# A two-layer decoder trunk: the comparison before a seldom-needed second path becomes a jump, and four engines get a branch hint

## The chip, the cores and the metric

The kernel runs on one core of one Trainium2 chip. The metric is the device time of one execution in microseconds (us). A core has five engines, each with an instruction stream of its own: TensorE (PE in the profile, with its weight loads as PEld), VectorE (DVE), ScalarE (ACT), GpSimd (POOL) and SyncE (SP). Names with a q at the end (SPq, DVEq, PEldq) are the engines' sequencers, which issue DMAs, wait on semaphores, load registers and branch.

## The reference, cut to what matters

`reference()` runs two pre-norm residual layers over 1024 tokens of width 1024, each followed by a SwiGLU feed-forward block, and a final RMSNorm. Layer 0 mixes tokens by a Conformer convolution and an mLSTM; layer 1 by gated linear attention:

```python
for l in range(DEPTH):                      # DEPTH = 2
    h = rmsnorm(x, mix_norm_g[l])
    if l % 2 == 0:
        x = x + conv_mlstm_mixer(h, ...)
    else:
        x = x + gla_mixer(h, ...)           # S_t = diag(alpha_t) S_{t-1} + k_t^T v_t, o_t = q_t S_t
    h = rmsnorm(x, ffn_norm_g[l])
    x = x + swiglu(h, ffn_w1[l], ffn_w3[l], ffn_w2[l])
return rmsnorm(x, final_norm_g)
```

The decays alpha_t of layer 1 come from the data. Their running sums of logarithms decide which of two ways of computing layer 1 can be used.

## The kernel before, in words

Everything is float32, carried by pairs of a rounded value and its remainder, so that each product is three matmuls (`mm3`, L174 to L176). The sequence is cut in two halves of 512 tokens; activations lie as 8 tiles of 128 features by 512 tokens. The feed-forward blocks use a seven-product scheme for 2x2 blocks. The order of the work within an engine comes from the Tile scheduler, steered by priorities and by the lists `ORDER0`, `ORDER1`, `FIRST` and `REST`.

The program is one long straight piece, with a branch near its end:

- `layer(0, mixer0, ...)` (L1844) computes layer 0, and its `done` writes the layer's result to `x1` in DRAM.
- `layer(1, ... mixer1_at_once ...)` (L1845) computes layer 1 under the assumption that the decays of a chunk of 128 tokens stay above a bound. `compare()` (L1058 to L1066) tests that and leaves 1 or 0 in the one-element tile `fits`. The final norm is done by `finish` (L1764) for the first 768 tokens and by `last_tokens` (L1774) for the last 256, whose output is stored at L1834 and L1837 by DMAs on SP's and ACT's queues.
- `nc.values_load(fits, ...)` (L1846) loads `fits` into a register on all five engines (TENSOR_LOAD in the profile).
- `with tc.If(ok < 1, preferred_fallthrough_block=False)` (L1847): if the assumption fails, layer 1 is computed again from `x1` by the slower `mixer1`, and the output is overwritten. This is the long arm. With the given inputs `fits` is 1, and the long arm doesn't run.

An `If` has two arms. The short arm, which the code doesn't write, holds what keeps the semaphores' counts alike on both ways: on PE, DVE, ACT and POOL one semaphore instruction each, on SP eight, one for each of the eight DMA semaphores that this program uses in turn. Each waits until that semaphore has the count of all work issued so far, and then adds what the long arm would have added. On SP these eight thus wait until the last output DMAs have landed. All of them carry L1847 in the profile.

Behind both arms comes the end of the program, under L1971 (the line that closes the `TileContext`): on SP eight waits and a drain, then a barrier of all five engines led by POOL, which clears the semaphores, and a second barrier.

Before the change the streams lie in memory as: straight piece, short arm, long arm, end. An engine for which `fits` is 1 does not jump at the comparison, runs the short arm, and jumps from there over the long arm to the end. Both the comparison and that jump appear as COMPARE_BRANCH under L1847.

Of the kernel before, what the change touches and what calls it, by code (L numbers as in the profile page):

```python
# [79 lines left out]
def trunk_kernel(ctx, tc, xT, cols, gate_b0, ev_vo0, ev_u, ev_cw, ev_out, od_v0, od_u, od_out, gate_w2, fin_row,  # L80
# [57 lines left out]
    def xy(i, half):  # L138
        return hp.tile([P, HALF], F32, tag=f"xy{i}_{half}", name=nm(f"xy{i}"))
# [86 lines left out]
    def norm_half(xs, gc, half):  # L226
        r = rstd_half(xs)
        hs, work = [], []
        for k in range(KT):
            f = tmp()  # L230
            a = DVE.scalar_tensor_tensor(out=f, in0=xs[k], scalar=c1(gc + k), in1=r, op0=ALU.mult, op1=ALU.mult)
            d = hl(k, half)
            work += [[a], [split(d, f, DVE)]]
            hs.append(d)
        return hs, work
# [18 lines left out]
    def out_proj(wd, x_src):  # L254

        ys = [[None] * KT, [None] * KT]
        second = []

        def cut(y, half, ks=range(KT)):
            for k in ks:  # L260
                if ys[half][k] is None:
                    ys[half][k] = hl(k, half)
                    y(k, half, ys[half][k], second if half and k >= 2 else None)

        def run(y, half, done, mp=None):
            if half == 0:
                cut(y, 0)
            x = []
            for i in range(KT):
                w = spare(wd[i], mp) if mp and i in XW else weights(wd[i], 1024, DVE, off=OOFF)  # L270
                if half == 0 and i == 1:
                    second[:] = made
                t = xy(i, half)
                SP.dma_start(t, x_src[i, half])
                x.append(t)
                b = proj(w, ys, half)
                DVE.tensor_tensor(out=t, in0=t, in1=b, op=ALU.add)
            if half == 0:
                cut(y, 1)
            with tc.high_priority(offset=NOFF):  # L280
                done(x, half)
        return run, cut
# [1444 lines left out]
    def layer(l, mixer, w_out, x_src, g, done):  # L1727
        hv, d = ffn_in(g)
        run, cut = out_proj(w_out, x_src)
        ys = []  # L1730

        def then(y, mp):
            ys.append(y)
            run(y, 0, d, mp if l == 0 else None)

        mixer(cut, then)
        with tc.tile_pool(name=f"u{l}", bufs=1, reuse_waits="tile") as fp:
            pools.append(fp)
            run(ys[0], 1, d)
            ffn_up(l, hv, fp)  # L1740
            ffn_down(l, fp, done)
# [101 lines left out]
    h1, b1, done = before(C_MIX + 8)  # L1843
    layer(0, mixer0, ev_out, xT, C_FFN, done)  # L1844
    layer(1, lambda cut, then: mixer1_at_once(h1, b1, cut, then), od_out, x1, C_FFN + 8, finish)  # L1845
    ok = nc.values_load(fits, min_val=0, max_val=1, skip_runtime_bounds_check_because="a comparison gives 0 or 1")  # L1846
    with tc.If(ok < 1, preferred_fallthrough_block=False):  # L1847
        h = []
        for half in range(2):
            xs = [xy(k, half) for k in range(KT)]  # L1850
            for k in range(KT):
                SP.dma_start(xs[k], x1[k, half])
            h.append(norm_half(xs, C_MIX + 8, half)[0])
        layer(1, lambda cut, then: mixer1(h, cut, then), od_out, x1, C_FFN + 8, finish)
# [96 lines left out]
def _build(a):  # L1951
    import concourse.bacc as bacc

    nc = bacc.Bacc("TRN2", target_bir_lowering=False, num_devices=1, dynamic_dma_scratch_size=2048)
    args = [nc.dram_tensor(f"in_{k}", v.shape, mybir.dt.from_np(v.dtype), kind="ExternalInput").ap() for k, v in a.items()]
    args.append(nc.dram_tensor("out_0", (KT, 2, P, HALF), F32, kind="ExternalOutput").ap())
    args.append(nc.dram_tensor("xsp", (KT, 2, P, HALF), F32, kind="Internal").ap())
    md = {n: [nc.dram_tensor(f"md{n}_{k}", (P, HALF), F32, kind="Internal").ap() for k in range(11)]
          for n in ("B11", "B21", "B22", "T1", "T2", "T3", "T4")}
    args.append(nc.dram_tensor("rowd", (2, HEADS, T), F32, kind="Internal").ap())  # L1960
    args.append([nc.dram_tensor(f"ud_{k}", (P, PH, NT), F32, kind="Internal").ap() for k in range(4)])
    args.append(nc.dram_tensor("zd", (32, CG, PH, NT), F32, kind="Internal").ap())
    args.append(nc.dram_tensor("ad", (LEAD, 2, P, HALF), F32, kind="Internal").ap())
    args.append(nc.dram_tensor("x1", (KT, 2, P, HALF), F32, kind="Internal").ap())
    args.append(nc.dram_tensor("cd", (8, 2, P, HALF), F32, kind="Internal").ap())
    args.append(nc.dram_tensor("cv", (2, P, HALF), F32, kind="Internal").ap())
    args.append(nc.dram_tensor("td", (3, 4, P, HALF), F32, kind="Internal").ap())
    args.append(nc.dram_tensor("vd", (2, 2, P, 1024), F32, kind="Internal").ap())
    args.append(nc.dram_tensor("yd", (4, 2, P, HALF), F32, kind="Internal").ap())
    args.append(nc.dram_tensor("bd", (HEADS, 2, P, HALF), F32, kind="Internal").ap())  # L1970
    with tile.TileContext(nc, schedule_with_timeline_sim=True) as tc:  # L1971
        trunk_kernel(tc, *args, md)
    return nc
# [14 lines left out]
```

## Time and profile before

| what | us |
|---|---|
| median of 3 runs | 2112.68 |
| lowest and highest | 2112.63, 2113.97 |
| the profiled execution's own time | 2114.76 |
| its span, first to last instruction of the program | 2113.0 |

| engine | busy us | share of the span | instructions |
|---|---|---|---|
| PE | 2094.4 | 99% | 10367 |
| DVE | 1508.1 | 71% | 2296 |
| ACT | 866.7 | 41% | 1411 |
| POOL | 2.9 | 0% | 15 |

Busy time counts compute instructions alone: semaphore waits, register loads, branches and DMA issues are not in it. A row of a line's view gives engine, operation and count, the shortest, median and longest duration in ns, and where the first and the last of them start, in us from the start of the span. A row of the DMA view gives a queue, its kind, packets, MB and the share of 16 DMA engines' time; the queues of the kind "instruction" bring in the engines' own code.

### The profile page before, as it was taken

The page shows a single profiled execution, that of the slowest core. Times are in us where ns is not written, and L with a number is a line of the kernel's source. Part 1 is how long each engine was busy: PE and PEld are TensorE (multiplying, and loading weights), DVE is VectorE, ACT ScalarE, POOL GpSimd, SP SyncE. Part 2 cuts the span into 40 slices and gives each one's busy share as a digit, 9 for nine tenths or more (in the row PEclk, how much of TensorE's full clock was granted, in tenths as well). Part 3 has the DMA queues.
Part 4 walks back from the last instruction along what each step waited for, and adds up shares of the span by engine and source line. Part 5 has one row for each costly group of instructions (what it writes and reads, how often), then busy time and mean ns, then how long its engine had stood idle before and what let it go on. Part 6 is the DMA issues. An engine that isn't in the chain of part 4 may idle for free.

```text
span 2113.0 us, 27851 instructions
## 1 busy us (share of the span) xinstructions
PE 2094.4 (99%) x10367; PEld 1773.1 (84%) x10367; DVE 1508.1 (71%) x2296; ACT 866.7 (41%) x1411; POOL 2.9 (0%) x15
## 2 busy tenths in 40 slices
PE   9999999999999999999999999999999999999998
PEld 8889989888888888888889978888888888888887
DVE  7555788677776666867876577667877666677696
ACT  6302327443222222444546546744522222235553
POOL 0000000000000000000000000000000000000000
PEclk9999999999999999999999999999999999999999
DMA  4233453555443233834436643554544333374334
GB/s 162 91 107 126 148 131 119 204 170 180 163 157 105 90 113 134 287 97 138 161 127 229 200 141 115 175 184 140 195 155 164 113 116 103 103 285 129 98 122 146
DMA packets 154640, 312.61 MB, mean 148 GB/s; under 512 B 24128, under 2 KB 37312, under 8 KB 154496
## 3 DMA queue, kind: packets, MB, share of 16 engines
q1 hardware_dynamic: 154224, 310.48, 43.9%
q8 instruction: 84, 1.38, 0.3%
q14 instruction: 60, 0.49, 0.1%
q10 hardware_dynamic: 272, 0.26, 0.0%
HBM read 229.91 MB, written 80.77 MB: 147 GB/s over the span
## 4 chain that ended last, share of the span: by engine, by line
PE 94%; DVE 2%; ACT 2%; DMA 1%; issue 0%; SPq 0%; DVEq 0%; ACTq 0%
PE mm L174 20%; PE mm L175 20%; PE mm L176 20%; PE sm L175 10%; PE sm L176 10%; PE sm L174 10%; PE sm L411 2%; PE sm L1266 1%; PE sm L1268 1%; PE sm L1265 1%; DVE bs L1053 0%; DVE hL L147 0%; DVE wL L168 0%; PE sm L1254 0%; PE sm L1293 0%
## 5 line engine op out<-in xcount | busy, mean ns | idle before, releaser
L175 PE MATMUL mm<-hL,wH 128*128 128x512 f32 x1356 | 531.2, 392 | 0.2 <-DVE hL L339 0.2
L176 PE MATMUL mm<-hH,wH 128*128 128x512 f32 x1356 | 529.1, 391 | 0.0
L174 PE MATMUL mm<-hH,wL 128*128 128x512 f32 x1356 | 492.5, 392 | 2.4 <-DVE wL L168 1.4
L174 PEld LDWEIGHTS mm<-hH,wL 128*128 128x128 f32 x1356 | 254.3, 188 | 57.6 <-ACT hH L338 1.3
L175 PEld LDWEIGHTS mm<-hL,wH 128*128 128x128 f32 x1356 | 254.7, 188 | 53.3 <-DVE hL L339 1.0
L176 PEld LDWEIGHTS mm<-hH,wH 128*128 128x128 f32 x1356 | 254.7, 188 | 53.1 <-issue 0.2
L175 PE MATMUL sm<-hL,wH 128*128 128x512 f32 x616 | 240.1, 390 | 0.0
L176 PE MATMUL sm<-hH,wH 128*128 128x512 f32 x616 | 239.7, 389 | 0.0
L174 PE MATMUL sm<-hH,wL 128*128 128x512 f32 x616 | 209.0, 390 | 0.0
L147 ACT ACTIVATE wH<-S 128x1024 fp32r<-128x1024 f32 x97 | 102.8, 1060 | 233.8 <-PE sm L176 214.5
L147 ACT ACTIVATE wH<-q 128x512 fp32r<-128x512 f32 x143 | 90.3, 632 | 178.8 <-PE mm L176 101.3
L147 DVE TENSOR_TENSOR wL<-q,wH 128x512 fp32r<-128x512 f32 x143 | 98.5, 689 | 71.5 <-ACT wH L147 71.0
L147 ACT ACTIVATE wH<-raw 128x1024 fp32r<-128x1024 f32 (+1 forms) x90 | 90.0, 1001 | 118.7 <-PE sm L176 67.3
L147 DVE TENSOR_TENSOR wL<-S,wH 128x1024 fp32r<-128x1024 f32 x97 | 118.4, 1221 | 26.3 <-ACT wH L147 26.3
L175 PEld LDWEIGHTS sm<-hL,wH 128*128 128x128 f32 x616 | 115.6, 188 | 24.7 <-issue 0.7
L174 PEld LDWEIGHTS sm<-hH,wL 128*128 128x128 f32 x616 | 115.6, 188 | 24.5 <-PE mm L176 0.5
L175 PE MATMUL mm<-wL,hH 128*128 128x256 f32 (+2 forms) x480 | 136.0, 284 | 0.0
L176 PEld LDWEIGHTS sm<-hH,wH 128*128 128x128 f32 x616 | 115.6, 188 | 24.2 <-issue 0.2
L176 PE MATMUL mm<-wH,hH 128*128 128x256 f32 (+2 forms) x480 | 135.9, 285 | 0.0
L174 PE MATMUL mm<-wH,hL 128*128 128x256 f32 (+2 forms) x480 | 135.8, 286 | 0.1
L1493 DVE TENSOR_TENSOR c<-sm,c 128x512 f32<-128x512 f32 x110 | 75.6, 687 | 72.5 <-PE sm L176 72.5
L147 DVE TENSOR_TENSOR wL<-raw,wH 128x1024 fp32r<-128x1024 f32 (+1 forms) x90 | 103.3, 1149 | 13.9 <-ACT wH L147 13.8
(355 smaller groups left out, 3579.2 us busy)
## 6 DMA issues: line engine op xcount, KB each, us to landing
raw<-in_w SPq DMA_DIRECT2D x108, 512.0 KB
mdT<-c SPq DMA_DIRECT2D x88, 256.0 KB
m<-mdT SPq DMA_DIRECT2D x88, 256.0 KB
mdB<-c SPq DMA_DIRECT2D x66, 256.0 KB
raw<-in_od_u SPq DMA_DIRECT2D x32, 512.0 KB
q<-in_w SPq DMA_DIRECT2D x60, 256.0 KB
m<-mdB SPq DMA_DIRECT2D x55, 256.0 KB
raw<-in_ev_u SPq DMA_DIRECT2D x20, 512.0 KB
```

What stands on the lines that cost most here:

```text
L147: ins = ACT.activation(dst[0], src, AF.Copy), lo.tensor_tensor(out=dst[1], in0=src, in1=dst[0], op=ALU.subtract)
L174: return (PE.matmul(o, lt[1], rt[0], start=start and not on, stop=False, skip_group_check=on), PE.matmul(o, lt[0], rt[1], start=False, sto ...
L175: PE.matmul(o, lt[0], rt[1], start=False, stop=False, skip_group_check=on),
L176: PE.matmul(o, lt[0], rt[0], start=False, stop=stop, skip_group_check=on))
L411: PE.matmul(o, w[:, m * P:(m + 1) * P], raw[:, e, m:m + NT], start=m == 0, stop=m == SH)
L1265: PE.matmul(db[:, cc, :], kw[:, cs], v[:, c, :], start=True, stop=True)
L1266: PE.matmul(ob[:, cc, :], A[:, cs], v[:, c, :], start=True, stop=st is None)
L1268: PE.matmul(ob[:, cc, :], q[:, cs], st, start=False, stop=True)
L1493: DVE.tensor_tensor(out=out, in0=a, in1=b, op=ALU.add)
```

## The change

```diff
     layer(0, mixer0, ev_out, xT, C_FFN, done)
     layer(1, lambda cut, then: mixer1_at_once(h1, b1, cut, then), od_out, x1, C_FFN + 8, finish)
+    tc.mark_branch_hint_location("redo", hint="LikelyTaken", engines=[mybir.EngineType.SP, mybir.EngineType.Activation, mybir.EngineType.DVE, mybir.EngineType.PE])
     ok = nc.values_load(fits, min_val=0, max_val=1, skip_runtime_bounds_check_because="a comparison gives 0 or 1")
-    with tc.If(ok < 1, preferred_fallthrough_block=False):
+    with tc.If(ok < 1, preferred_fallthrough_block=True, label="redo"):
         h = []
```

The streams now lie as: straight piece, long arm, short arm, end. The comparison is turned round: an engine for which `fits` is 1 jumps over the long arm to the short arm, and the end follows the short arm directly. On SP, ACT, DVE and PE a BRANCH_PREFETCH_HINT instruction names the comparison's branch and says that it is likely taken. POOL gets none. From here on a line of the changed kernel has a number one higher than before, from L1846 on.

This is the part of SP's stream around the comparison before: the last three output DMAs (L1837, L1834), the load of `fits`, the comparison, the short arm's jump, and the first loads of the long arm. Semaphore instructions are not shown.

```order
L1837 DMA out<-xy_3395_17971 128x2x256
L1834 DMA out<-xy_3397_17977 128x256 x2
L1846 TENSOR_LOAD fits
L1847 COMPARE_AND_BRANCH
L1847 UNCONDITIONAL_BRANCH
L164 DMA raw_18388<-in_od_u 128x1024
L164 DMA raw_18394<-in_od_v 128x1088
```

And this is the same place of SP's stream in the changed kernel.

```order
L1837 DMA out<-xy_3395_17971 128x2x256
L1834 DMA out<-xy_3397_17977 128x256 x2
L1847 TENSOR_LOAD fits
L1848 COMPARE_AND_BRANCH
L164 DMA raw_18392<-in_od_u 128x1024
L164 DMA raw_18398<-in_od_v 128x1088
```

The long arm's first load now follows the comparison. The short arm and its jump have moved behind the long arm, at whose end two jumps now stand in a row where one stood: the long arm's, over the short arm, and the short arm's, whose target is what follows it.

The hint was written ahead of the load of `fits`, but carries no dependency that would hold it there. This piece of the difference is the head of SP's stream.

```order
-L1971 UNCONDITIONAL_BRANCH
+L1972 UNCONDITIONAL_BRANCH
+L1972 BRANCH_PREFETCH_HINT
 L114 DMA col<-in_cols 128x136
 L319 DMA raw_119<-in_ev_u 128x512
```

The hint stands at the very top, ahead of the first DMA, and likewise ahead of the first instruction of PE, DVE and ACT. Between it and the comparison lies the whole straight piece: some 1800 instructions on SP, 3000 on DVE, 2000 on ACT and 10,200 on PE, each engine's in the order of before.

## The prediction

> **What bounds the kernel now.** I read the page first, then the stage table of the last 33 us, then the two lines of the branch and of the program's end on SP, and the DMA view over the stretch between them. The kernel as a whole is bound by TensorE:
>
> ```profile
> PE 2094.4 (99%) x10367; PEld 1773.1 (84%) x10367; DVE 1508.1 (71%) x2296; ACT 866.7 (41%) x1411; POOL 2.9 (0%) x15
> ```
>
> The change touches none of that work. It touches what comes after it, and the stage table shows how long that is:
>
> ```profile
> 2080.00:2102.90 22.90, 22.87 (x131) 19.80 (x129) 13.18 (x34) 7.26 (x15) 0.00 (x0) 1.00 0.30 97
> 2102.90:2105.30 2.40, 0.00 (x0) 0.00 (x0) 1.41 (x5) 1.70 (x4) 0.00 (x0) 1.00 0.58 193
> 2105.30:2113.00 7.70, 0.00 (x0) 0.00 (x0) 0.00 (x0) 0.00 (x0) 0.00 (x0) 0.58 0.24 77
> ```
>
> The columns after the stretch and its length are the busy us of PE, PEld, DVE, ACT and POOL. TensorE is done at 2102.9 and the last DVE result at 2105.3; then no engine computes for 7.7 us. SP runs through this stretch like this: it loads `fits`, compares, passes five semaphore waits at once, three more after a hold, jumps, and later reaches the end.
>
> ```profile
> L1846 SPq TENSOR_LOAD <-fits x1: 798/798/798, 2105.8 to 2105.8; - x1
> L1847 SPq COMPARE_BRANCH  x1: 49/49/49, 2106.7 to 2106.7; - x1
> L1847 SPq EVENT_SEMAPHORE  x5: 17/17/17, 2106.8 to 2107.1; - x5
> L1847 SPq EVENT_SEMAPHORE  x3: 17/17/17, 2108.6 to 2108.8; - x3
> L1847 SPq COMPARE_BRANCH  x1: 43/43/43, 2108.9 to 2108.9; - x1
> L1971 SPq EVENT_SEMAPHORE  x10: 17/28/28, 2111.6 to 2112.9; - x10
> L1971 SPq DRAIN  x3: 7/7/13, 2112.2 to 2112.5; - x3
> ```
>
> Two pieces of waiting stand out. Between 2107.1 and 2108.6 SP waits for the last output DMAs to land, 1.5 us. Between the jump at 2108.9 (43 ns long) and the first instruction of the end at 2111.6 lie 2.7 us in which SP has nothing to wait for but its own code. The DMA view over 2108.85 to 2111.7 shows that in this time the chip moved instructions and nothing else:
>
> ```profile
> DMA packets 3, 0.02 MB, mean 9 GB/s; under 512 B 0, under 2 KB 0, under 8 KB 0
> q14 instruction: 3, 0.02, 2.7%
> ```
>
> So the jump's 2.7 us are a fetch of code from where the jump goes. The other engines pay the same price at their jumps, earlier:
>
> ```profile
> L1847 PEldq COMPARE_BRANCH  x2: 95/1914/3732, 2099.5 to 2103.1; - x2
> L1847 DVEq COMPARE_BRANCH  x2: 51/53/55, 2105.0 to 2105.4; - x2
> L1847 ACTq COMPARE_BRANCH  x2: 38/43/48, 2106.3 to 2106.4; - x2
> L1971 PEldq DRAIN  x2: 8/40/73, 2106.9 to 2112.6; - x2
> L1971 DVEq DRAIN  x2: 10/25/40, 2109.0 to 2112.5; - x2
> L1971 ACTq DRAIN  x2: 8/44/81, 2109.3 to 2112.5; - x2
> ```
>
> The DMA view over 2103 to 2106.9 shows the code that PE waited for, by another queue:
>
> ```profile
> q8 instruction: 1, 0.02, 1.5%
> ```
>
> PE's jump at 2103.1 is itself 3732 ns long; DVE goes from its jump at 2105.4 to its first drain at 2109.0 (3.5 us after the jump's 51 ns), ACT from 2106.4 to 2109.3 (2.8). All three stand at the final barrier by 2109.3. SP comes there at 2112.2. Its chain, landing wait, jump, fetch, eight waits, barrier, sets the end of the program.
>
> **The change part by part.** The sum is made against the profiled execution (2114.76 us, span 2113.0), which lies 2.08 us above the median of 2112.68; the difference it gives is then taken from the median. About 0.2% (4.2 us) is what a measurement of this kernel can tell from no change.
>
> *The short arm's jump goes away.* Its target now follows it. That a jump to the next instruction costs nothing is borne out by the one at the head of the program: the order has an UNCONDITIONAL_BRANCH under L1971 on SP, while the trace's only rows of L1971 on SP are the semaphore and drain rows above. In SP's chain the eighth wait starts at 2108.8, and the first wait of the end would then follow at the pace of the waits, (2107.1 - 2106.8) / 4 = 0.075 us, at about 2108.9 instead of 2111.6. That is 2.7 us off the path that sets the end, if the arm and the end come in with one fetch.
>
> *The comparison becomes a jump, which needs that fetch.* SP compares at 2106.7. If the hint does what it says, the code is there when SP jumps. The trace has no jump whose target is there already; the nearest rows are a comparison that falls through (49 ns) from below and SP's 2.7 us, or PE's 3.7, from above. I take the low end for the hinted case, since a fetch ahead of time has all of the kernel to hide in. What covers a slower jump is the landing wait: up to 1.5 us on SP cost nothing, because the DMAs land at 2108.6 whenever SP begins to wait. So the low end, and anything up to 1.5 us, has price zero. Without the cover it would count in full.
>
> *What is late next.* With SP's fetch gone, SP stands at the barrier about 0.6 us after 2108.9 (from 2111.6 to 2112.2 above), at 2109.5. With hints the other three are there by about 2106.6 (ACT, which compares at 2106.3). Without hints DVE would fetch from 2105.1 to 2108.6 and ACT from 2106.3 to 2109.1, still ahead of 2109.5. PE compares at 2099.5, while its queue still holds matmuls until 2102.9, and a 3.7 us fetch there ends at 2103.2. POOL has no hint, but has long passed its comparison:
>
> ```profile
> L1847 POOLq COMPARE_BRANCH  x2: 38/42/45, 1324.1 to 1324.3; - x2
> ```
>
> The landing wait is the new bound of the tail, and it is not touched.
>
> *The hints.* One more instruction at the top of four streams, ahead of SP's first DMA, on which the first real matmul depends by way of the loads. The trace has no such instruction. Its bounds are SP's cheapest row (a drain, 7 ns) and its dearest register instruction (the 798 ns load of `fits`); I take 0.05 us, the size of the branch records (43 and 49 ns), which it is nearest to. A cost below nothing is excluded: the first DMA can only move later.
>
> [...]
>
> *The sum.* Minus 2.7, plus 0, plus 0.05: minus 2.65 us. The span would be 2110.35, the profiled execution 2112.1, and the median 2112.68 - 2.65 = 2110.0.
>
> **The rivals.**
>
> *The hint does nothing, the fetch only moves.* Placed some 1800 instructions ahead of SP's comparison, the hint may be forgotten by then. SP then stalls at 2106.7 + 0.05 for 2.7 us, until 2109.45. By then all DMAs have landed, so the eight waits pass at 0.075 us each, 0.6 us in all, and the end begins at 2110.05 instead of 2111.6: 1.55 us gained, 1.5 after the hint's own 0.05, since the fetch now runs beside the landing wait instead of behind it. Time 2111.2. With PE's 3.7 us as the stall the end begins at 2111.05, the gain is 0.5 and the time 2112.2. For it speaks the distance; against it, that the hint names its branch. Chance 0.25. [...]
>
> *No gain at all.* The arm and the end could come in with two fetches instead of one. Then SP stalls again behind the arm, as it does now: with a working hint the time stays at 2112.68 + 0.05 = 2112.7, and without one it is about 2.7 above the previous rival, 2113.9. Against it stand the page's counts of such packets:
>
> ```profile
> q8 instruction: 84, 1.38, 0.3%
> q14 instruction: 60, 0.49, 0.1%
> ```
>
> PE's 84 packets make 1.38 MB for twice 10367 instructions, some 67 bytes each; a q14 packet of 0.49 MB / 60, or 8 KB, then holds about 120 instructions, and the arm and the end on SP are nine and thirteen by the rows above. But a piece can lie across an edge. Chance 0.08. [...]
>
> *Slower: the armed hint takes room from the ordinary fetches.* If the hint makes each sequencer bring in the target at the top and hold it for the whole kernel, less room is left for the code that comes next, and each step to the next piece of code can stall. The 60 packets of q14 belong to SP, DVE and ACT (POOL with its 15 instructions hardly counts), some 20 each. At 2.7 us a stall, 20 stalls cost such an engine 54 us; with DVE idle for 29% of the span most of this would be absorbed, and if a third showed, the time would be 2112.7 + 18 - 2.7 = 2128. It decides from the point where more than 4.2 + 2.7 = 6.9 us show: two of PE's fetches at 3.7 us, or three of DVE's on PE's path. A single mistaken fetch at the top, 2.7 to 3.7 us, would only cancel the gain. Against it: PE's sequencer runs ahead of its engine (it compared 3.4 us before the last matmul ended), which hides most of one stall; and a hint that names one far branch has no reason to act on others. Chance 0.04.
>
> **How the numbers follow.** Forecast with a working hint 0.60; the moved fetch 0.25; no gain 0.08; slower 0.04; the remaining 0.03 for a gain above 4.2 us, for which I know of no mechanism: the whole stretch behind the landing wait is 2113.0 - 2108.6 = 4.4 us, and the waits and barriers stay. The predicted time is that of the likeliest case, 2110.0. The range goes up to 2112.2, the slow bound of the moved fetch, and down to 2109.0, less than the 1.34 us by which the three runs of before lie apart. It leaves out the no-gain, slow and very fast cases, 0.15. All cases but the last two lie within 0.2% of the time before: same 0.93, faster 0.03, slower 0.04.
>
> **What would show it.** In the profile of the changed kernel SP's comparison (now L1848) should be followed within 0.3 us by the first of eight waits; the last wait of the arm and the first of the end (L1972) should lie 0.1 us apart, with no second COMPARE_BRANCH on SP. The landing wait should still end near 2108.6, and the span near 2110.4. If the hint does nothing, the gap of 2.7 us stands right behind the comparison, and the eight waits follow at 0.075 us. If code comes in by two fetches, a gap over 1 us stands between the arm and the end. The slow rival would show in the q8 and q14 counts (well above 84 and 60) and in waits early in the kernel. A tail that begins later than 2105.3, or a gain above 4.2 us, would say that I have the mechanism wrong.

## The result, and the profile after

| | median us | lowest, highest | runs |
|---|---|---|---|
| before | 2114.98 | 2112.63, 2116.32 | 22 |
| changed | 2111.49 | 2109.53, 2114.05 | 22 |

The ratio is 0.9986, with a 95% interval of 0.9980 to 0.9992: between 1.7 and 4.2 us faster, 3.0 us in the middle (the two medians alone lie 3.5 us apart). That is within the 0.2% of the forecast, and clear of zero. The forecast of 2110.0 stood on three runs of before with a median of 2112.68; in the longer comparison before lies 2.3 us higher, so the change is the better measure: -2.65 us forecast, -3.0 measured. The times alone hardly part the forecast from the rival in which the fetch only moves: 2111.49 lies nearer to that rival's 2111.2, and the 1.5 us that it would gain lie just below the interval. The profile parts them.

The stage table of the changed kernel's profile (stretch, length, busy us of PE, PEld, DVE, ACT and POOL, then clock and DMA), with the last row again from the last DVE result to the end:

```profile
2103.90:2106.30 2.40, 0.00 (x0) 0.00 (x0) 1.41 (x5) 1.69 (x4) 0.00 (x0) 1.00 0.68 229
2106.30:2110.90 4.60, 0.00 (x0) 0.00 (x0) 0.00 (x0) 0.00 (x0) 0.00 (x0) 0.66 0.37 119
```

The stretch with no engine at work has gone from 7.7 us to 4.6. In this execution the work before it ended 1.0 us later than in the profile of before; the same place lies between 2104.8 and 2106.6 in the nine profiles of this study, hinted or not, so one pair of spans says less than the tails. I call tail the time from the end of the last DVE result (L1832) to the end of the span, 7.7 us before. SP in the tail, by its rows at the load of `fits` (now L1847), the branch (L1848, the eight waits in two windows) and the end (L1972):

```profile
L1847 SPq TENSOR_LOAD <-fits x1: 686/686/686, 2107.3 to 2107.3; - x1
L1848 SPq COMPARE_BRANCH  x1: 70/70/70, 2108.0 to 2108.0; - x1
L1848 SPq EVENT_SEMAPHORE  x5: 17/17/17, 2108.5 to 2108.9; - x5
L1848 SPq EVENT_SEMAPHORE  x3: 17/17/17, 2109.1 to 2109.5; - x3
L1972 SPq EVENT_SEMAPHORE  x10: 17/28/28, 2109.6 to 2110.8; - x10
L1972 SPq DRAIN  x3: 7/7/13, 2110.1 to 2110.4; - x3
```

There is one COMPARE_BRANCH on SP where there were two. The first wait follows it after 0.5 us, where a jump without a hint took 2.7, and from the arm's last wait at 2109.5 to the end's first at 2109.6 is one step. The other engines:

```profile
L1848 PEldq COMPARE_BRANCH  x1: 4316/4316/4316, 2100.5 to 2100.5; - x1
L1848 DVEq COMPARE_BRANCH  x1: 84/84/84, 2106.0 to 2106.0; - x1
L1848 DVEq EVENT_SEMAPHORE  x1: 21/21/21, 2106.6 to 2106.6; - x1
L1848 ACTq COMPARE_BRANCH  x1: 68/68/68, 2107.3 to 2107.3; - x1
L1848 ACTq EVENT_SEMAPHORE  x1: 17/17/17, 2107.8 to 2107.8; - x1
```

DVE and ACT are in their short arms 0.6 and 0.5 us after they begin to compare. The trace of packets shows that DVE's code was already there: no q14 code packet starts between 2074.8 and 2107.2, and DVE is in its arm at 2106.6. PE isn't so quick: its comparison, hinted like the others, is 4316 ns long. The page's counts of code packets have gone down a little, from 84 and 60:

```profile
q8 instruction: 83, 1.36, 0.3%
q14 instruction: 57, 0.47, 0.1%
```

And at the head, SP's hint takes 56 ns and its first DMA starts at 0.92 us, where before it started at 0.81:

```profile
L1972 SPq BRANCH_PREFETCH_HINT  x1: 56/56/56, 0.8 to 0.8; - x1
0.92 0.41 SPq L114 DMA_DIRECT2D col<-in_cols  x1
```

### The profile page after: what moved, and what is told of

Same layout as the page of the kernel before. It is cut to its first block, busy times and chain, and to the rows that moved or that the text cites. A ratio compares the mean times of both kernels' runs of the same rounds, so it can differ in the third digit from the quotient of the medians.

```text
span 2110.9 us, 27850 instructions
## 1 busy us (share of the span) xinstructions
PE 2094.3 (99%) x10367; PEld 1773.9 (84%) x10367; DVE 1508.4 (71%) x2296; ACT 866.7 (41%) x1411; POOL 2.9 (0%) x15
## 3 DMA queue, kind: packets, MB, share of 16 engines
q8 instruction: 83, 1.36, 0.3%
## 4 chain that ended last, share of the span: by engine, by line
PE 96%; ACT 1%; DVE 1%; DMA 1%; issue 0%; SPq 0%; DVEq 0%; ACTq 0%
PE mm L174 20%; PE mm L175 20%; PE mm L176 20%; PE sm L176 10%; PE sm L174 10%; PE sm L175 10%; PE sm L411 2%; PE sm L1266 1%; PE sm L1268 1%; PE sm L1265 0%; DVE bs L1053 0%; PE sm L624 0%; PE sm L1293 0%; PE sm L1254 0%; PE sm L591 0%; PE sm L626 0%
```

## The experiments

The theory: SP alone sets the end. Moving the arm lets SP's fetch of code run beside the landing wait, and SP's hint takes the fetch away. Rivals: all of the gain is the hint's; or every engine's fetch counts; or the gain lies in the straight piece, whose code has moved by one instruction. The tails below are the span less the end of the last DVE result, each from one profile.

| kernel | last DVE result ends | span | tail | ratio to before, 95% |
|---|---|---|---|---|
| before | 2105.28 | 2113.0 | 7.7 | |
| changed | 2106.27 | 2110.9 | 4.6 | 0.9986 (0.9980 to 0.9992) |
| changed, once more | 2105.39 | 2110.1 | 4.7 | one run, no ratio |
| no hint | 2105.18 | 2111.8 | 6.6 | 0.9992 (0.9983 to 1.0001) |
| hint on SP alone | 2106.63 | 2111.5 | 4.9 | 0.9990 (0.9980 to 0.9999) |
| hint on the other three | 2106.39 | 2112.4 | 6.0 | 0.9992 (0.9983 to 1.0001) |
| old order, four hints | 2104.83 | 2112.5 | 7.7 | 0.9997 (0.9987 to 1.0006) |
| no branch at all | 2105.68 | 2109.1 | 3.4 | 0.9976 (0.9967 to 0.9985) |
| PE's code moved | 2106.36 | 2111.0 | 4.6 | 0.9996 (0.9987 to 1.0005) |

A ratio is to the runs of before that were measured together with that kernel. The intervals are too wide to part neighbours in this table; the tails part them.

**The moved arm without hints.**

```diff
-    tc.mark_branch_hint_location("redo", hint="LikelyTaken", engines=[...])
-    with tc.If(ok < 1, preferred_fallthrough_block=True, label="redo"):
+    with tc.If(ok < 1, preferred_fallthrough_block=True):
```

> The changed kernel without its four hints: the short arm still stands behind the long one and falls into the end. I call tail the time from the end of the last DVE result (L1832) to the end of the span: 7.7 us before, 4.7 after. Theory (SP's fetch sets the end; the moved arm lets the fetch run beside the landing wait, the hint removes it): SP fetches for 2.7 us right behind its comparison, then passes eight waits at 0.08 us, and the tail is 6.1 us; time 1.5 us below before, ratio 0.9993. Rival (all of the gain is the hint's): the tail is 7.7 us, ratio 1.000. Rival (the gain lies in the straight piece, whose code was shifted by one instruction): tail anything, ratio 1.000, since the shift is gone.

SP's rows of the branch (L1847 here) and of its last two output DMAs (L1834):

```profile
L1847 SPq COMPARE_BRANCH  x1: 50/50/50, 2107.3 to 2107.3; - x1
L1847 SPq EVENT_SEMAPHORE  x8: 17/17/17, 2109.9 to 2110.4; - x8
L1834 SPq DMA_DIRECT2D out<-xy x2: 345/885/1425, 2104.8 to 2105.3; - x2
```

The fetch stands where the theory puts it, 2.6 us right behind the comparison, and the eight waits then pass within 0.5 us. That the hint brings all of the gain is thereby refuted in the profile: the tail is 1.1 us shorter than before without any hint. It is 6.6 us and not 6.1, because SP reached its comparison late: the second of its last two DMAs took 1425 ns to issue, where it took 383 before. More on that below.

**A hint on SP alone, and on the other three alone.**

```diff
-    ... engines=[mybir.EngineType.SP, mybir.EngineType.Activation, mybir.EngineType.DVE, mybir.EngineType.PE])
+    ... engines=[mybir.EngineType.SP])                                    # the one kernel
+    ... engines=[mybir.EngineType.Activation, mybir.EngineType.DVE, mybir.EngineType.PE])  # the other
```

> The changed kernel with the hint on SP alone. Theory: DVE, ACT and PE fetch at their comparisons (2.7 to 4.3 us), but reach the final barrier no later than SP, so that the tail stays at 4.7 us (up to 4.9, since ACT compares about 0.8 us ahead of SP and a fetch of 2.8 us brings it to the barrier within 0.1 us of SP); ratio 0.9987. Rival (every engine's fetch counts): tail about 6 us, ratio 0.9993.

> The changed kernel with the hint on ACT, DVE and PE, not on SP. Theory: as without any hint, SP fetches for 2.7 us behind its comparison; tail 6.1 us, ratio 0.9993. Rival (every engine's fetch counts, or the hints' place in the stream): tail 4.7 to 5.5 us, ratio 0.9987 to 0.9990.

The first has a tail of 4.9 us, the second one of 6.0. In the first, DVE and ACT have fetched (3.4 and 2.9 us from the comparison to the arm), and reach their drains at 2109.9 and 2110.5 (the first starts in these rows), while SP's first drain starts at 2110.7:

```profile
L1972 DVEq DRAIN  x2: 10/14/17, 2109.9 to 2111.1; - x2
L1972 ACTq DRAIN  x2: 8/8/8, 2110.5 to 2111.0; - x2
L1972 SPq DRAIN  x3: 7/7/13, 2110.7 to 2111.0; - x3
```

In the second, SP stalls as without hints, from 2107.9 to 2110.5:

```profile
L1848 SPq COMPARE_BRANCH  x1: 50/50/50, 2107.9 to 2107.9; - x1
L1848 SPq EVENT_SEMAPHORE  x8: 17/17/17, 2110.5 to 2111.1; - x8
```

So only SP's hint acts on the end. The other three gain at most the 0.2 us between 4.9 and 4.7. That 0.2 us lies in the landing: the last wait of SP's arm starts 3.5 us after the last DVE result with SP's hint alone, and 3.2 to 3.3 in the two profiles of the changed kernel.

**The old order with the hints.**

```diff
-    with tc.If(ok < 1, preferred_fallthrough_block=True, label="redo"):
+    with tc.If(ok < 1, preferred_fallthrough_block=False, label="redo"):
```

> The kernel before with the four hints added: the short arm again comes first and jumps over the long arm, so the hinted comparison isn't taken. Theory: a hint that doesn't come true gains nothing, the jump from the short arm fetches as before; tail 7.7 us, ratio 1.000. If the hinted target is brought in instead of what follows, engines whose short arm lies across an edge of code fetch twice: then up to 2.7 us more, tail 10.4 us, ratio 1.0013. Rival (one more instruction at the head shifts the code of the straight piece and that is the gain): ratio 0.9986.

The tail is 7.7 us, that of before, and the ratio 0.9997. SP falls through, jumps at 2108.4, and has its first instruction of the end at 2111.2:

```profile
L1848 SPq COMPARE_BRANCH  x2: 53/63/73, 2106.3 to 2108.4; - x2
L1972 SPq EVENT_SEMAPHORE  x10: 17/28/28, 2111.2 to 2112.4; - x10
```

The one-instruction shift of the straight piece is thus not the gain, and a hint that doesn't come true cost nothing here that the tail shows.

**No branch.** This kernel leaves out the second way of computing layer 1, the comparison and the load of `fits`.

```diff
-    ok = nc.values_load(fits, ...)
-    with tc.If(ok < 1, ...):
-        ...
```

> The kernel without the load of fits, the comparison and both arms: layer 1 is computed once and the program ends. It leaves out the second way of computing layer 1 (not needed for these inputs). Theory (behind the fetch, the landing of the last output DMAs bounds the tail): the eight waits of the end now are the landing wait; against the changed kernel only the short arm's eight waits of 0.07 us go, so the tail is 4.1 to 4.2 us, against 4.7 with the hinted branch and 7.7 before; ratio 0.9984. Rival (the hinted branch still costs a fetch or a register load on the path): tail below 3.5 us.

The tail is 3.4 us, under the bound that the rival set, not the 4.1 to 4.2 of the theory. SP's last DMA began to issue 0.10 us after the last DVE result in both kernels. It took 384 ns here and 852 in the changed kernel, but that isn't the reason for what follows: with PE's code moved (below) it took 382 ns, and the arm's last wait started 3.2 us after the last DVE result all the same. Without the branch the waits for these DMAs ended sooner: SP's first drain, which follows the last of these waits, starts at 2108.4 or 2.7 us after the last DVE result, where the changed kernel's last wait in the short arm starts 3.2 us after it (2109.5) and the same drain 3.8 us (2110.1).

```profile
L1962 SPq EVENT_SEMAPHORE  x8: 17/28/28, 2106.2 to 2109.0; - x8
L1962 SPq DRAIN  x3: 7/7/7, 2108.4 to 2108.7; - x3
```

The DMA view from 2.3 us after the last DVE result on shows what comes late. Without the branch (2108.0 to 2109.1) nothing moves any more; in the changed kernel (2108.6 to 2109.5) eight packets of the output are still to come, in before (2107.6 to 2108.8) ten. Code packets run beside them:

```profile
DMA packets 0, 0.00 MB, mean 0 GB/s; under 512 B 0, under 2 KB 0, under 8 KB 0
```

```profile
q14 instruction: 1, 0.01, 3.2%
q1 hardware_dynamic: 8, 0.01, 2.5%
```

```profile
q8 instruction: 1, 0.02, 6.6%
q1 hardware_dynamic: 7, 0.01, 2.1%
q10 hardware_dynamic: 3, 0.00, 1.3%
```

A packet is counted where it starts. The code packet in the view of the changed kernel starts at 2109.1, when the last of the eight (2108.96) is through; the one that runs beside them started at 2108.35 and stands in the view from 2108.0 to 2108.9:

```profile
q14 instruction: 1, 0.01, 3.3%
```

So of the 1.2 us between the tails some 0.5 are the short arm's eight waits, as the theory has it, and some 0.6 an earlier landing, which it did not have. In that the rival was right: the hinted branch still has a price on the path. SP shows no stall for it, though. The eight packets come late and strictly one after another, some 0.04 us each, as if a single DMA engine, held before by a code packet, were still at work while the others were done. That reading is argued from which kernels have it; the trace doesn't tell DMA engines apart, and no run here took the code packets alone away: the kernel without the branch also lacks the loads of `fits`.

**PE's code moved by 16 instructions.**

```diff
-WARM = 5
+WARM = 1
```

> The changed kernel with 1 warm-up matmul on PE instead of 5, which moves PE's code forward by 16 instructions, for the sake of PE's comparison: with its hint it still took 4316 ns, and its code packet started 1.0 us after the comparison did. Theory A (a hint fetches when the sequencer enters the piece of code that holds the branch, and on PE that edge lies a few instructions ahead of the comparison, too late): now the comparison lies ahead of that edge, PE's comparison takes under 0.3 us and reaches its short arm within 0.6 us, and SP's DMA issues of 0.85 to 0.87 us in the tail fall back to 0.4. Theory B (the hint doesn't work on PE, or not over 20,000 instructions): comparison again 3.7 to 4.5 us. Either way PE is off the path: tail 4.5 to 4.8 us, time as the changed kernel, ratio 0.9986, but for what fewer warm-up matmuls cost at the head.

Here PE's comparison, with the same hint, is 405 ns long (a little over the 0.3 us expected), and SP's last two pairs of DMAs issue in 0.34 to 0.50 us each (in the changed kernel one of each pair took 870 and 852 ns):

```profile
L1848 PEldq COMPARE_BRANCH  x1: 405/405/405, 2100.6 to 2100.6; - x1
L1834 SPq DMA_DIRECT2D out<-xy x2: 344/363/382, 2106.0 to 2106.5; - x2
L1837 SPq DMA_DIRECT2D out<-xy x2: 382/443/504, 2102.8 to 2103.3; - x2
```

So the hint does work on PE, and over 20,000 instructions, matmuls and their weight loads counted apart. The q8 packets, PE's code, fit theory A. In the changed kernel one starts at 2079.4 and the next at 2101.46, 1.0 us after the comparison began. Here they start at 2079.7 and 2102.5, so that what PE jumped to at 2100.6 had been there for 20 us. Theory B is refuted, unless PE's jump got quick by the move alone: no run moved the code without PE's hint.

That PE would be in its short arm within 0.6 us can't be read here: its semaphore instruction starts at 2104.0, as PE's last matmul ends (2103.95), and so it did in before (2102.9). The tail is 4.6 us all the same, as expected for an engine off the path. The ratio of 0.9996 misses the expected 0.9986, though the intervals touch (0.9987 to 1.0005 and 0.9980 to 0.9992); whether fewer warm-up matmuls cost the difference at the head was not taken apart, and stays open.

**The changed kernel once more.**

> The changed kernel once more, for how far a tail repeats: every theory expects the tail within 0.2 us of 4.65, SP from its comparison to its first wait in 0.4 to 0.6 us, and PE's comparison near 4 us.

Its tail is 4.7 us, SP goes from its comparison to its first wait in 0.5 us, PE's comparison is 4276 ns long. A tail repeats to 0.1 us where whole spans differ by 0.8.

No version that computes the same has a shorter tail or a lower ratio than the changed kernel. What is left in its tail over no branch at all is 4.6 - 3.4 = 1.2 us.

## Why the prediction was right, point by point

- *A jump costs a fetch of code, 2.7 us on SP, and SP sets the end.* Right. The fetch moves with the jump (2.6 us behind the comparison without a hint on SP, in two kernels) and goes with SP's hint alone. On SP, ACT, DVE and PE every jump without a hint took between 2.6 us (SP) and 5.0 (PE, no hints); with one it took 0.4 to 0.6, but for PE's in the kernels where its code wasn't moved (4.1 to 4.3).
- *The short arm's jump is free once its target follows.* Right: one step of 0.07 us. Its 2.7 us is the main term.
- *Any delay at the comparison up to 1.5 us has price zero.* Right in kind, with less cover than assumed. The hinted jump took 0.5 us where the forecast had the low end of 49 ns, and 0.3 as the sign to look for. The prediction says that the trace has no jump whose target is there already. It has one: POOL jumps at 1324.3, in the row that the prediction shows, and is at its first drain 0.45 us later, with no code packet between.

  ```profile
  L1971 POOLq DRAIN  x3: 34/82/117, 1324.8 to 2112.7; - x3
  ```

  By this row the low end was too low by 0.4 us. The landing wait covered that, but SP came 0.3 us later to its comparison (2108.0 - 2106.27 = 1.7 us after the last DVE result, 1.4 before), since its last DMA issued in 852 ns instead of 383. Of the 1.5 us some 0.4 were left as waiting: the arm's last wait started at 2109.5, where the pace of the first five (2108.5 to 2108.9) would have given 2109.1 to 2109.2.
- *The landing wait isn't touched.* Wrong by a size. The arm's last wait started 3.5 us after the last DVE result before (2108.8 - 2105.28) and 3.2 after (2109.5 - 2106.27). The DMAs still set the end of the wait, but not at the same place. These 0.3 us are missing from the sum: -2.7 - 0.3 + 0.1 = -2.9, beside the tail's -3.1 and the ratio's -3.0.
- *The hints cost 0.05 us.* The instruction did (50 to 56 ns in the changed kernel), but SP's first DMA starts there at 0.92 us instead of 0.81, 0.11 us later.
- *With hints the other three arrive early.* Right for DVE and ACT, wrong for PE, whose hint came to nothing; it had no price, because PE was through at 2105.0 (its 4316 ns end at 2104.8), before DVE's last result at 2106.27, as the prediction worked out for a PE without a hint.
- *The rivals.* The moved fetch is what the kernel does without SP's hint: 6.0 and 6.6 us of tail against a forecast of 7.7 - 1.55 = 6.15; the second is long by the slow DMA issue. The second fetch between arm and end did not occur. The slow rival, fetches displaced through the kernel, is refuted by the packet counts, 83 and 57, which went down.

## What to carry to other kernels

The branch that wasn't taken was not free here, because the short way behind it had to jump later (2.7 us on SP): put the arm that runs right before the code that follows both, so that there is one jump, and hint that jump on the engine whose arrival ends the program. Look for such a price in the gap between a branch and the next instruction of the same sequencer, with instruction packets alone in the DMA view; the branch's own row of 38 to 55 ns doesn't show it on SP, DVE and ACT. For a gain of 3 us among runs that spread by 4, compare the stage that was changed, not the spans.

## What the runs showed that I had not expected

- A hint at the very top still worked over 1800 to 3000 instructions on SP, DVE and ACT, and over 20,000 on PE. That it needs the comparison to lie well behind an edge of the code that is fetched in one piece (on PE a packet of q8, 1.36 MB / 83, or 16 KB) is my estimate, and rests on two places: PE's hinted comparison took 4316 and 4276 ns in one place and 405 ns 16 instructions earlier.
- An engine's code packets seem to slow others down. In four profiles of three kernels the second of SP's last two DMA issues took 0.85 to 1.43 us instead of 0.38: the changed kernel twice (852 and 1024 ns), the one without hints (1425) and the one with SP's hint alone (871). In each the trace has a code packet of PE beside that issue, and the issue ends 0.4 to 0.5 us after the packet does (in the changed kernel the packet runs from 2105.80 to 2106.76, the issue ends at 2107.22); where PE's packet came 0.2 us or more sooner (the old order, the hint on the other three, and before, where it runs from 2104.42 to 2105.35 and the issue begins at 2105.39) or much sooner (PE's code moved), it took 0.38 to 0.44. The last packets of the output, too, ended 0.5 us later in the changed kernel, with code packets beside them, than without the branch (2.7 and 2.2 us after the last DVE result). Both are readings of which kernels have it; no run isolates them.
